# One core, two transformer blocks in fp32: block 2's attention as a pipeline over query tiles, filter taps on ScalarE and adding DMAs

## The chip, the cores and the metric

The kernel runs on one core of a Trainium2 chip. The metric is the device time of one execution in microseconds. Three runs of the kernel before took 1311.97, 1314.42 and 1315.54 us; the median, 1314.42 us, is the time before. PE is TensorE, DVE VectorE, ACT ScalarE, POOL GpSimd, SP SyncE; PSUM is the memory that matmuls write, in eight banks of 512 fp32 columns per partition.

## The reference

Two blocks follow one another on a sequence of 512 tokens, 1024 wide, in fp32. The change lies in the mixer of block 2, whose input is `u = h @ w_in`, 2560 columns, cut into four parts of which each gives 256 columns of the output:

```python
y_a = conformer_conv_mixer(u_conf, ...)   # val * sigmoid(gate), 31-tap causal depthwise convolution,
                                          # group norm over 4 x 64 channels, silu
y_b = short_conv_mixer(u_sc, ...)         # b * (3-tap convolution of c * x)
y_c = moba_attention(u_att)               # 4 heads of 64, causal, softmax with a slope per head on the distance
y_d = rglru_mixer(u_lru, ...)             # 4-tap convolution, two block-diagonal gates, a = exp(log_a),
                                          # mult = sqrt(1 - a*a), linear recurrence over tokens, times gelu(gate)
y = jnp.concatenate([y_a, y_b, y_c, y_d], axis=-1) @ w_out
```

With 512 tokens there are two blocks of 256 keys and one past block is always chosen, so the attention is plain causal attention.

## The kernel before

Every fp32 operand of a large product is split into a high and a low half of type fp32r (`split`, line 111: ACT copies the high half, DVE subtracts it to get the low half), and a product is three matmuls: high with high, high with low, low with high (lines 138 to 140, 223 to 227). A projection "chunk" gives 128 columns of `u`, channels on the partitions and 512 tokens in the free dimension: eight k-steps of three matmuls into one PSUM bank (`cm_phase`), and an `evac` function that reads the bank. The weight of a chunk is split when its turn comes (`split_w`, `wh` and `wl`, five buffers). Weights come in blocks of 256 columns on SP's queue, into three `raw` buffers.

In the mixer the eight PSUM banks have roles: three for products (`mm`, used in turn: 0, 1, 2), two for scores (`s`), two for transposes (`pt`), one for the weighted sum (`o`). H3 is the split input of the output projection, eight chunks of 128 channels: 0 and 1 the 31-tap convolution, 2 and 3 the short one, 4 and 5 the attention, 6 and 7 the recurrence.

Order of the program: five chunks (two gates and two values of the convolution, the first gelu gate); then four chunks for queries and keys and a token-major product for the values (`tm_block`); then the four heads. `at_head` goes over the four tiles of 128 queries: two matmuls of scores, DVE adds slope and mask and takes the maximum, ACT takes Exp with its sum, DVE the reciprocal and the scaling (line 1187), PE transposes the tile block by block into PSUM, and DVE or ACT copies it to `apts` (line 1191). The weighted sum follows, four fp32 products per head (line 1241). After each head some of the remaining nine chunks run (`cuts`), after heads 0 and 1 one of the two recurrences (`lru`), after head 2 the convolution's mean, after head 3 its norm.

The 62 taps of the 31-tap convolution (2 x 128 channels) are DVE instructions that wait in a list, `bg`; `pump(n)` puts n of them into the program behind a chunk. The recurrence's product of `a` with itself is written into the PSUM tile of the gate (line 1164).

The program is not run in this order. The framework lists the instructions of each engine by a planner that simulates the program and takes, among the instructions whose inputs are there in the simulation, the one that was traced first; semaphores then keep the data right. An engine runs its own list in order. `tc.keep_in_program_order(ins)`, new in the change, puts `ins` behind the instruction that was traced before it on the same engine.

Behind the mixer comes the output projection (`tm_phase`, lines 1284 and 1285): all eight banks, two per tile of 128 tokens, tiles 0 and 1 first, k-chunks in the order 6, 7, 2, 3, 4, 5, 0, 1.

Of the kernel before, what the change touches and what calls it, by code (L numbers as in the profile page):

```python
# [8 lines left out]
F32 = mybir.dt.float32  # L9
F32R = mybir.dt.float32r  # L10
AF = mybir.ActivationFunctionType
OP = mybir.AluOpType
# [3 lines left out]
P = 128  # L16
T = 512
NT = T // P
D = 1024
KC = D // P  # L20
# [6 lines left out]
NEG = -1.0e30  # L27
# [14 lines left out]
def tile_two_blocks(ctx: ExitStack, tc: tile.TileContext, a: dict, out: bass.AP, dbg=None):  # L42
# [3 lines left out]
    def open_pool(name, side="left", space=None, bufs=1):  # L46
        kw = {"space": space} if space is not None else {"side": side}
        return tc.alloc_tile_pool(name=name, bufs=bufs, reuse_waits="tile", **kw)

    def bcast_rows(ap, n):  # L50
        return bass.AP(tensor=ap.tensor, offset=ap.offset, ap=[[0, n]] + [list(d) for d in ap.ap])
# [30 lines left out]
    ident = consts.tile([P, P], F32, name="ident")  # L82
# [69 lines left out]
    def pump(n):  # L152
        for _ in range(min(n, len(bg))):
            bg.pop(0)()
# [872 lines left out]
    for g in range(2):  # L1027
        pool.memset(gmean[64 * g:64 * g + 64, 64 * g:64 * g + 64], 1.0 / 64.0)
    def tmp():
        return mx.tile([P, T], F32, name="tmp", tag="tmp", bufs=6)  # L1030

    zp = [mx.tile([P, 30 + T], F32, name=f"zp{c}") for c in range(2)]
    th_g = {}
# [19 lines left out]
    def aq_evac(c):  # L1053
        def f(ps):
            for e in range(2):
                q, r = aq(2 * c + e), HALF[e]
                act.activation(q[r, :], ps[r, :], AF.Copy, scale=qscale[r, c:c + 1])
                dve.scalar_tensor_tensor(q[HALF[1 - e], :], ps[r, :], qscale[r, c:c + 1], q[r, :].bitcast(F32),
                                         op0=OP.mult, op1=OP.subtract)
        return f  # L1060

    def ak_evac(c):
        def f(ps):
            for e in range(2):
# [7 lines left out]
    cs, cx = {}, {}  # L1072

    def sc_c(c):
        def f(ps):
            cs[c], cx[c] = tmp(), tmp()
            act.activation(cs[c], ps, AF.Copy)
        return f

    def sc_x(c):  # L1080
        def f(ps):
            dve.tensor_mul(cx[c], cs[c], ps)
            w = pv[:, c, SCW:SCW + 3]
            act.activation(cs[c], cx[c], AF.Copy, scale=w[:, 2:3])
            for j in (1, 0):
                s = 2 - j
                dve.scalar_tensor_tensor(cs[c][:, s:], cx[c][:, :T - s], w[:, j:j + 1], cs[c][:, s:],
                                         op0=OP.mult, op1=OP.add)
        return f

    def sc_b(c):
        def f(ps):
            dve.tensor_mul(cx[c], cs[c], ps)
            split(H3[0][:, 2 + c, :], H3[1][:, 2 + c, :], cx[c])
        return f

    gl = {}
# [15 lines left out]
    lg = col_blocks(w_in2, 2304, 256)  # L1113
    acc = [mx.tile([P, T], F32, name=f"cacc{c}") for c in range(2)]

    def taps(c):
        z, w = zp[c], half[:, c, :]
        bg.append(lambda: dve.tensor_scalar(acc[c], z[:, 0:T], w[:, 0:1], pv[:, c, DWB:DWB + 1],
                                            op0=OP.mult, op1=OP.add))
        for j in range(1, 31):  # L1120
            bg.append(lambda j=j: dve.scalar_tensor_tensor(acc[c], z[:, j:j + T], w[:, j:j + 1], acc[c],  # L1121
                                                           op0=OP.mult, op1=OP.add))

    sq, var = {}, {}

    def conf_mean():
        for c in (1, 0):
# [20 lines left out]


    def lru(c):  # L1150
        ths, lps = [], []
        for i in range(2):
            ps = psm.tile([P, T], F32, name="lps", tag="mm", bufs=3)
            pe.matmul(ps, bd[:, i, c, :], xc[c], start=True, stop=True)
            th = tmp()
            act.activation(th, ps, AF.Tanh, scale=0.5, bias=lbh[:, c, i:i + 1])
            ths.append(th)
            lps.append(ps)
# [12 lines left out]
        split(H3[0][:, 6 + c, :], H3[1][:, 6 + c, :], xc[c])  # L1171

    def at_head(h):
        pts = m2.tile([P, NT, T], F32, name="apts", tag="apts", bufs=1)
        for i in range(NT):
            n = (i + 1) * P
            s = psm.tile([P, T], F32, name="as", tag="s", bufs=2)
            m = max(n, 256)
            for j in range(2):
                pe.matmul(s[:, :m], aq(h)[:, i * P:(i + 1) * P], ak(h)[j][:, :m], start=j == 0, stop=j == 1)  # L1180
            L = m2.tile([P, T], F32, name="aL", tag="aL", bufs=2)
            st = m2.tile([P, 3], F32, name="ast", tag="ast", bufs=4)
            dve.tensor_tensor_reduce(L[:, :n], s[:, :n], ab[:, T - n:], scale=-0.25 ** (h + 1), scalar=-NEG,
                                     op0=OP.add, op1=OP.min, accum_out=st[:, 0:1])
            act.activation(L[:, :n], L[:, :n], AF.Exp, scale=-1.0, bias=st[:, 0:1], accum_out=st[:, 1:2])
            dve.reciprocal(st[:, 2:3], st[:, 1:2])
            dve.tensor_scalar(L[:, :n], L[:, :n], st[:, 2:3], None, op0=OP.mult)
            pt = psm.tile([P, NT, P], F32, name="apt", tag="pt", bufs=2)
            for kb in range(i + 1):
                pe.transpose(pt[:, kb, :], L[:, kb * P:(kb + 1) * P], ident)  # L1190
            (act.copy if i % 2 else dve.tensor_copy)(pts[:, 0:i + 1, i * P:(i + 1) * P], pt[:, 0:i + 1, :])
        return pts
# [4 lines left out]
    for c in (1, 0):  # L1197
        taps(c)
    dump("x3", X)
    lnp.release()  # L1200
    psm = Banks(mm=(0, 1, 2), s=(3, 4), pt=(5, 6), o=(7,))
# [10 lines left out]
    akp = m2.tile([P, 2, 2, T], F32R, name="akp")  # L1212

    def aq(h):
        return H3[h % 2][:, 4 + h // 2, :]

    def ak(h):
        return [H3[i][:, h, :] if h < 2 else akp[:, h - 2, i, :] for i in range(2)]

    av = m2.tile([P, NT, 256], F32, name="av")  # L1220
    def av_evac(t0, ps):
        act.activation(av[:, t0:t0 + 2, :], ps.rearrange("p (u c) -> p u c", u=2), AF.Copy)
        pump(RATE)

    RATE = 5
# [3 lines left out]
    rest = chunks[5:]  # L1229
    for c in range(2):  # L1230
        rest += [(sc[c], sc_c(c)), (sx[c], sc_x(c)), (sb[c], sc_b(c))]
    cuts = (0, 3, 4, 6, len(rest))


    for c in range(2):
        o = psm.tile([P, T], F32, name="ao", tag="o", bufs=1)
        for e in range(2):
            h = 2 * c + e
            pts = at_head(h)
            for kb in range(NT):  # L1240
                pe.matmul(o[64 * e:64 * e + 64, kb * P:], av[:, kb, h * 64:(h + 1) * 64], pts[:, kb, kb * P:],
                          start=kb == 0, stop=kb == NT - 1)
            cm_phase(*MM, rest[cuts[h]:cuts[h + 1]], X3, 0, rate=RATE)
            if h in (0, 1):
                lru(h)
            if h == 2:
                pump(len(bg))
                conf_mean()
            if h == 3:
                conf_norm()  # L1250
        split(H3[0][:, 4 + c, :], H3[1][:, 4 + c, :], o)
    dump("h3h", H3[0].bitcast(F32))
    m2.release()
    mx.release()
# [145 lines left out]
```

## Time and profile before

| | |
|---|---|
| median of 3 runs | 1314.42 us (1311.97 to 1315.54) |
| the profiled execution | 1314.05 us, span 1312.3 us |
| PE busy | 1294.6 us (99%), 6856 matmuls |
| DVE, ACT, POOL busy | 744.0 us (57%), 533.6 us (41%), 79.3 us (6%) |
| granted TensorE clock | 0.997 of full speed |
| block 2's mixer | 754 to 904 us of the span; its output projection 904 to 952.7 |

A profile shows one execution. Busy time is the time in which an engine works on an instruction; matmuls overlap one another, so the time from one start to the next is what a matmul costs. "Idle before" is time in which an engine stood still before an instruction, and what ended that idle time stands behind the arrow. Shares are of the whole span; what bounds a stretch has to be read from the stretch.

### The profile page before, as it was taken

The page shows a single profiled execution, that of the slowest core. Times are in us where ns is not written, and L with a number is a line of the kernel's source. Part 1 is how long each engine was busy: PE and PEld are TensorE (multiplying, and loading weights), DVE is VectorE, ACT ScalarE, POOL GpSimd, SP SyncE. Part 2 cuts the span into 40 slices and gives each one's busy share as a digit, 9 for nine tenths or more (in the row PEclk, how much of TensorE's full clock was granted, in tenths as well). Part 3 has the DMA queues.
Part 4 walks back from the last instruction along what each step waited for, and adds up shares of the span by engine and source line. Part 5 has one row for each costly group of instructions (what it writes and reads, how often), then busy time and mean ns, then how long its engine had stood idle before and what let it go on. Part 6 is the DMA issues. An engine that isn't in the chain of part 4 may idle for free.

```text
span 1312.3 us, 16931 instructions
## 1 busy us (share of the span) xinstructions
PE 1294.6 (99%) x6856; PEld 1107.5 (84%) x6856; DVE 744.0 (57%) x1202; ACT 533.6 (41%) x893; POOL 79.3 (6%) x152
## 2 busy tenths in 40 slices
PE   9999999999999999999999999899999999999998
PEld 8899899899889888888888898677898888888886
DVE  6765876576476655566533669996453334532432
ACT  5764464234333333344432234566432223431321
POOL 3220120110010000000000110000100000000000
PEclk9999999999999999999999999999999999999999
DMA  8322344534034332322223124112223332223211
GB/s 268 98 70 68 113 139 159 197 127 161 0 118 137 108 104 93 100 96 97 96 97 128 33 77 152 65 45 87 79 89 120 96 96 97 97 97 112 96 42 56
DMA packets 92447, 134.87 MB, mean 103 GB/s; under 512 B 4627, under 2 KB 77645, under 8 KB 92369
## 3 DMA queue, kind: packets, MB, share of 16 engines
q1 hardware_dynamic: 88560, 128.53, 29.7%
q10 hardware_dynamic: 3153, 3.14, 0.7%
q0 software_dynamic: 656, 2.12, 0.5%
q8 instruction: 54, 0.88, 0.3%
q14 instruction: 24, 0.20, 0.0%
HBM read 131.66 MB, written 2.12 MB: 102 GB/s over the span
## 4 chain that ended last, share of the span: by engine, by line
PE 92%; DVE 4%; ACT 1%; issue 1%; POOL 1%; DMA 0%; ACTq 0%; DVEq 0%; POOLq 0%
PE cm L139 15%; PE cm L138 15%; PE cm L140 15%; PE tm L223 9%; PE tm L224 9%; PE tm L227 9%; PE tmc L200 2%; PE tmc L201 2%; PE tmc L199 2%; PE tr L294 1%; PE tm L140 1%; PE tm L138 1%; PE tm L139 1%; DVE wl L113 1%; PE num L675 1%; DVE cacc L1121 1%
## 5 line engine op out<-in xcount | busy, mean ns | idle before, releaser
L113 DVE TENSOR_TENSOR wl<-rawc,wh 128x1024 fp32r<-128x1024 f32 x140 | 170.6, 1221 | 203.6 <-ACT wh L112 203.0
L112 ACT ACTIVATE wh<-rawc 128x1024 fp32r<-128x1024 f32 x140 | 147.8, 1059 | 244.7 <-PE cm L139 193.2
L113 DVE TENSOR_TENSOR wl<-rawr,wh 128x1024 fp32r<-128x1024 f32 x73 | 88.9, 1223 | 154.3 <-ACT wh L112 154.2
L112 ACT ACTIVATE wh<-rawr 128x1024 fp32r<-128x1024 f32 x73 | 77.0, 1059 | 182.6 <-PE tm L227 125.9
L139 PE MATMUL cm<-x2l,wh 128*128 128x512 f32 (+1 forms) x392 | 144.0, 368 | 0.0
L140 PE MATMUL cm<-x2h,wl 128*128 128x512 f32 (+1 forms) x392 | 143.8, 367 | 0.0
L138 PE MATMUL cm<-x2h,wh 128*128 128x512 f32 (+1 forms) x392 | 143.1, 368 | 0.0
L139 PE MATMUL cm<-x4l,wh 128*128 128x512 f32 (+1 forms) x296 | 106.6, 361 | 1.3 <-DVE x4l L113 1.3
L140 PE MATMUL cm<-x4h,wl 128*128 128x512 f32 (+1 forms) x296 | 106.4, 360 | 0.0
L138 PE MATMUL cm<-x4h,wh 128*128 128x512 f32 (+1 forms) x296 | 105.9, 361 | 0.0
L139 PEld LDWEIGHTS cm<-x2l,wh 128*128 128x128 f32 x392 | 73.8, 188 | 12.4 <-DVE x2l L113 0.2
L140 PEld LDWEIGHTS cm<-x2h,wl 128*128 128x128 f32 x392 | 73.8, 188 | 12.3
L138 PEld LDWEIGHTS cm<-x2h,wh 128*128 128x128 f32 x392 | 73.4, 188 | 12.0
L619 DVE SCALAR_TENSOR_TENSOR uy<-cm,fw,uy 128x511 f32<-128x511 f32 x88 | 65.5, 746 | 1.4
L138 PE MATMUL cm<-x3h,wh 128*128 128x512 f32 (+1 forms) x184 | 63.6, 351 | 1.1 <-DVE xc L619 0.8
L139 PE MATMUL cm<-x3l,wh 128*128 128x512 f32 (+1 forms) x184 | 64.3, 351 | 0.0
L139 PEld LDWEIGHTS cm<-x4l,wh 128*128 128x128 f32 x296 | 55.8, 189 | 9.9 <-DVE x4l L113 1.5
L140 PE MATMUL cm<-x3h,wl 128*128 128x512 f32 (+1 forms) x184 | 64.0, 349 | 0.0
L140 PEld LDWEIGHTS cm<-x4h,wl 128*128 128x128 f32 x296 | 55.8, 189 | 8.4
L138 PEld LDWEIGHTS cm<-x4h,wh 128*128 128x128 f32 x296 | 55.5, 189 | 8.4
L317 POOL TENSOR_TENSOR rs_r<-rs_e,mhalf 128x1 f32<-128x1 f32 (+1 forms) x16 | 26.4, 1652 | 534.2 <-DVE rs_e L316 534.2
L200 PE MATMUL tmc<-wl,xh 128*128 128x256 f32 (+1 forms) x160 | 46.6, 291 | 0.7 <-DVE wl L113 0.7
(460 smaller groups left out, 3037.3 us busy)
## 6 DMA issues: line engine op xcount, KB each, us to landing
rawc<-in_ffn_w_up_dram SPq DMA_DIRECT2D x22, 1024.0 KB
rawc<-in_w_in_dram SPq DMA_DIRECT2D x20, 1024.0 KB
rawc<-in_mlp_w_dram SPq DMA_DIRECT2D x16, 1024.0 KB
rawr<-in_mlp_w_dram SPq DMA_DIRECT2D x16, 1024.0 KB
rawr<-in_ffn_w_down_dram SPq DMA_DIRECT2D x11, 1024.0 KB
rawr<-in_w_out_dram SPq DMA_DIRECT2D x10, 1024.0 KB
rawc<-in_xa_wkv_dram SPq DMA_DIRECT2D x8, 1024.0 KB
rawc<-in_xa_wq_dram SPq DMA_DIRECT2D x4, 1024.0 KB
```

The source lines that it names most:

```text
L112: act.activation(hi, src, AF.Copy)
L113: dve.tensor_sub(lo, src, hi.bitcast(F32))
L138: pe.matmul(ps, wh, xh, start=first, stop=False)
L139: pe.matmul(ps, wh, xl, start=False, stop=False)
L140: pe.matmul(ps, wl, xh, start=False, stop=last)
L199: pe.matmul(o, xh, wh, start=k == 0, stop=False)
L200: pe.matmul(o, xh, wl, start=False, stop=False)
L223: pe.matmul(ps[t][h], xh, wh[:, c], start=i == 0, stop=False)
L224: pe.matmul(ps[t][h], xh, wl[:, c], start=False, stop=False)
L227: pe.matmul(ps[t][h], xl, wh[:, c], start=False, stop=i == n - 1)
L317: pool.tensor_tensor(r, t, mhalf[:, :n], op=OP.pow)
L619: dve.scalar_tensor_tensor(dst[:, s:], ps[:, :T - s], w[:, j:j + 1], y[:, s:], op0=OP.mult, op1=OP.add)
```

## The change

- The attention becomes one loop over 16 units (4 heads x 4 query tiles). Unit u issues its scores, then its share of the 72 k-steps of the nine remaining chunks (`stream`, 4.5 per unit), then the transposes of unit u - 2, and at every second unit the weighted sum of the two tiles before. The scores, k-steps, transposes and sums are each kept in program order.
- The weights' scaling by the reciprocal moves from DVE to ACT. The transposed weights and the values are split in fp32r halves (ACT and DVE); the halves of a head's values lie side by side in 128 columns, so one matmul against the high weights and one against the low ones, of 256 columns, give four products; the two halves of the result are added by an ACT copy and a DVE addition of 64 partitions.
- The keys of heads 2 and 3 lie in chunks 2 and 3 of H3 instead of in `akp`, so the short convolution's last factor (`sb`) moves to the end of the stream. The chunks of the recurrence's input come first.
- Nine of the 31 taps of channels 128 to 255 become ACT copies with a scale, kept in program order, one after each of the four query and key chunks and each half of the values, one before them, two in units 0 and 2. The first writes `accd`; each of the other eight writes one of two `ctap` buffers, which a DMA from POOL's queue adds to `accd`. DVE adds `accd` to the other taps' sum before the mean.
- The recurrence's square is an ACT instruction into SBUF. `tmp` has five buffers, not six.
- The convolution's mean and norm stand behind the loop.

```diff
-        dve.tensor_mul(lps[0], av_, av_)
-        dve.scalar_tensor_tensor(tn, lps[0], 1.0, tn, op0=OP.add, op1=OP.mult)
+        a2 = tmp()
+        act.activation(a2, av_, AF.Square)
+        dve.scalar_tensor_tensor(tn, a2, 1.0, tn, op0=OP.add, op1=OP.mult)
...
+    NDMA = 8
+    accd = mx.tile([P, T], F32, name="caccd")
+
+    def act_tap(j):
+        z, w = zp[1], half[:, 1, :]
+        first = j == 30 - NDMA
+        t = accd if first else mx.tile([P, T], F32, name="ctap", tag="ctap", bufs=2)
+        in_order(act.activation(t, z[:, j:j + T], AF.Copy, scale=w[:, j:j + 1]))
+        if not first:
+            pool.dma_start(accd, t, accum_op=OP.add)
...
+    RATE = 6
     ATT = [(aqs[c], aq_evac(c)) for c in range(2)] + [(aks[c], ak_evac(c)) for c in range(2)]
-    cm_phase(*MM, ATT, X3, 0, rate=RATE)
+    for chunk in ATT:
+        cm_phase(*MM, [chunk], X3, 0, rate=4)
+        next_act_tap()
     tm_block(w_in2, 1792, X3, NT, *MM, av_evac)
+    rest = chunks[6:] + [chunks[5]] + [(sc[0], sc_c(0)), (sx[0], sc_x(0)), (sc[1], sc_c(1)), (sx[1], sc_x(1)),
+                         (sb[0], sc_b(0)), (sb[1], sc_b(1))]
+    def stream():
+        for n, (src, evac) in enumerate(rest):
+            w = split_w(src())
+            ps = psm.tile([P, T], F32, name="cm", tag="mm", bufs=3)
+            for k in range(KC):
+                for i, (wi, xi) in enumerate(((0, 0), (0, 1), (1, 0))):
+                    in_order(pe.matmul(ps, w[wi][:, k, :], X3[xi][:, k, :], start=k == 0 and i == 0,
+                                       stop=k == KC - 1 and i == 2))
+                if k == KC - 1:
+                    evac(ps)
+                if (n, k) in ((1, 3), (2, KC - 1)):
+                    lru(n - 1)
+                yield
...
+    def at_scores(h, i):
...
+        dve.reciprocal(st[:, 2:3], st[:, 1:2])
+        act.activation(L[:, :n], L[:, :n], AF.Copy, scale=st[:, 2:3])
+        Ls[h, i] = L
+
+    def at_turn(h, i):
+        L = Ls.pop((h, i))
+        pt = psm.tile([P, NT, P], F32, name="apt", tag="pt", bufs=2)
+        for kb in range(i + 1):
+            in_order(pe.transpose(pt[:, kb, :], L[:, kb * P:(kb + 1) * P], ident))
+        d = ptp[i // 2][:, :, 0:i + 1, (i % 2) * P:(i % 2 + 1) * P]
+        split(d[:, 0], d[:, 1], pt[:, 0:i + 1, :])
+
+    def at_sum(h, p):
+        if p == 0:
+            os_[h] = psm.tile([P, T], F32, name="ao", tag="o", bufs=1)
+        o = os_[h]
+        for kb in range(2 * p + 2):
+            for i in range(2):
+                in_order(pe.matmul(o[:, p * 256:(p + 1) * 256], av[:, kb, h, :], ptp[p][:, i, kb, :],
+                                   start=kb == 0 and i == 0, stop=kb == 2 * p + 1 and i == 1))
...
+    for u in range(N + 3):
+        if u < N:
+            at_scores(*units[u])
+        upto = min((u + 1) * len(rest) * KC // N, len(rest) * KC)
+        for _ in range(upto - done):
+            next(filler)
+        done = upto
+        if 2 <= u < N + 2:
+            at_turn(*units[u - 2])
+        if u >= 4 and u % 2 == 0:
+            at_sum(units[u - 3][0], units[u - 3][1] // 2)
+        if u in (0, 2):
+            next_act_tap()
+        pump(1 if u < 3 else 2)
+    for _ in filler:
+        pass
+    pump(len(bg))
+    conf_mean()
+    conf_norm()
```

## Rows read from the trace of the kernel before

**Rows 1.** Busy us of each engine in four stretches, then granted clock, DMA, GB/s.
```profile
786.00:824.60 38.60, 38.60 (x239) 34.84 (x238) 37.82 (x58) 21.03 (x31) 0.00 (x0) 1.00 0.41 136
824.60:904.00 79.40, 74.69 (x324) 55.21 (x322) 67.34 (x137) 44.50 (x76) 0.00 (x0) 0.98 0.20 67
904.00:952.70 48.70, 48.70 (x222) 39.18 (x221) 26.31 (x35) 27.32 (x51) 3.57 (x5) 1.00 0.28 86
...
860.00:870.00 10.00, 10.00 (x47) 7.74 (x46) 10.00 (x23) 8.76 (x15) 0.00 (x0) 1.00 0.30 103
```
**Rows 2.** PE's waits: waiting line, releaser, us in total, times, longest.
```profile
PE apt L1190 <- DVE aL L1187: 2.3, 1, 2.3
...
PE ao L1241 <- DVE apts L1191: 1.3, 1, 1.3
...
PE cm L138 <- DVE xc L619: 0.8, 1, 0.8
```
**Rows 3.** The stretch behind those waits: us, PE busy, granted clock, DMA, GB/s.
```profile
854.40:858.10 3.70, 3.70 (x10) 0.55 0.00 0
```
**Rows 4.** Timeline of PE: start, us, instruction; three pairs of neighbours.
```profile
871.12 2.37 PE L1241 MATMUL ao<-apts,av 128*64 128x512 f32 x8
873.42 0.91 PE L1180 MATMUL as<-akp,h3h 128*128 128x384 f32 x3
...
812.71 0.28 PE L199 MATMUL tmc<-wh,x3h 128*128 128x256 f32 x1
812.83 0.28 PE L200 MATMUL tmc<-wl,x3h 128*128 128x256 f32 x1
...
858.83 0.39 PE L138 MATMUL cm<-x3h,wh 128*128 128x512 f32 x1
859.06 0.39 PE L139 MATMUL cm<-x3l,wh 128*128 128x512 f32 x1
```
**Rows 5.** Groups by form from 824.6 to 904: busy us, mean ns | idle before.
```profile
L1121 DVE SCALAR_TENSOR_TENSOR cacc<-zp,half,cacc 128x512 f32<-128x512 f32 x29 | 20.7, 739 | 0.0
...
L1187 DVE TENSOR_SCALAR aL<-aL,ast 128x512 f32<-128x512 f32 x4 | 1.9, 478 | 0.0
...
L1084 ACT ACTIVATE tmp<-tmp,pv 128x512 f32<-128x512 f32 x2 | 1.4, 706 | 0.0
...
L1164 DVE TENSOR_TENSOR lps<-tmp 128x512 f32<-128x512 f32 x2 | 1.4, 685 | 0.0
...
L1187 DVE TENSOR_SCALAR aL<-aL,ast 128x128 f32<-128x128 f32 x3 | 0.8, 280 | 0.0
```
**Rows 6.** Timeline of ACT and DVE: the second four-tap convolution, first and last pass.
```profile
843.52 0.76 ACT L616 ACTIVATE xc<-cm,pv 128x512 f32<-128x512 f32 x1
...
853.60 0.74 DVE L619 SCALAR_TENSOR_TENSOR xc<-cm,pv,xc 128x509 f32<-128x509 f32 x1
```
**Rows 7.** Timeline of ACT: the second gelu gate.
```profile
832.42 1.28 ACT L1102 ACT_TABLE_LOAD   x1
833.72 0.60 ACT L1102 ACTIVATE tmp<-cm 128x512 f32<-128x512 f32 x1
```
**Rows 8.** DMA issues on POOL's queue: count, KB each, median us to landing.
```profile
swb<-vfwd_d POOLq DMA_DIRECT2D x1, 1024.0 KB, 9.1
...
mb<-mrow_d POOLq DMA_DIRECT2D x4, 256.0 KB, 3.5
```
**Rows 9.** Timeline of POOL: two powers on 128x1.
```profile
256.40 3.72 POOL L317 TENSOR_TENSOR rs_r<-rs_e,mhalf 128x1 f32<-128x1 f32 x1 [28.42 <-DVE rs_e L316]
...
930.31 0.54 POOL L980 TENSOR_TENSOR ssr<-ssv,mhalf 128x1 f32<-128x1 f32 x1 [156.80 <-PE tm L227]
```
**Rows 10.** Timeline of PE, DVE and ACT about the output projection's start.
```profile
902.68 1.88 PE L1137 MATMUL cva<-tmp,gmean 128*128 128x512 f32 x4
...
913.10 1.29 DVE L113 TENSOR_TENSOR h3l<-cacc,h3h 128x512 fp32r<-128x512 f32 x2
...
914.43 2.96 ACT L112 ACTIVATE wxh<-rawr 128x1024 fp32r<-128x1024 f32 x3
```

More of the change, by code (lines that the diff above doesn't have):

```diff
@@ L48, in open_pool @@
         return tc.alloc_tile_pool(name=name, bufs=bufs, reuse_waits="tile", **kw)
+    in_order = tc.keep_in_program_order
     def bcast_rows(ap, n):
@@ L1029, in tmp @@
     def tmp():
-        return mx.tile([P, T], F32, name="tmp", tag="tmp", bufs=6)
+        return mx.tile([P, T], F32, name="tmp", tag="tmp", bufs=5)
     zp = [mx.tile([P, 30 + T], F32, name=f"zp{c}") for c in range(2)]
@@ L1070, in ak_evac @@
         return f
-    cs, cx = {}, {}
+    cs = {}
     def sc_c(c):
         def f(ps):
-            cs[c], cx[c] = tmp(), tmp()
+            cs[c] = tmp()
             act.activation(cs[c], ps, AF.Copy)
@@ L1081, in f @@
         def f(ps):
-            dve.tensor_mul(cx[c], cs[c], ps)
+            cx = tmp()
+            dve.tensor_mul(cx, cs[c], ps)
             w = pv[:, c, SCW:SCW + 3]
-            act.activation(cs[c], cx[c], AF.Copy, scale=w[:, 2:3])
+            act.activation(cs[c], cx, AF.Copy, scale=w[:, 2:3])
             for j in (1, 0):
                 s = 2 - j
-                dve.scalar_tensor_tensor(cs[c][:, s:], cx[c][:, :T - s], w[:, j:j + 1], cs[c][:, s:],
+                dve.scalar_tensor_tensor(cs[c][:, s:], cx[:, :T - s], w[:, j:j + 1], cs[c][:, s:],
                                          op0=OP.mult, op1=OP.add)
@@ L1092, in f @@
         def f(ps):
-            dve.tensor_mul(cx[c], cs[c], ps)
-            split(H3[0][:, 2 + c, :], H3[1][:, 2 + c, :], cx[c])
+            dve.tensor_mul(cs[c], cs[c], ps)
+            split(H3[0][:, 2 + c, :], H3[1][:, 2 + c, :], cs[c])
         return f
@@ L1114, in tile_two_blocks, with next_act_tap, taps @@
     acc = [mx.tile([P, T], F32, name=f"cacc{c}") for c in range(2)]
[L1116 to L1122, printed above, removed]
+    NDMA = 8
[7 more added lines that the diff above has]
+            pool.dma_start(accd, t, accum_op=OP.add)
+    act_taps = iter(range(30 - NDMA, 31))
+    def next_act_tap():
+        for j in act_taps:
+            act_tap(j)
+            return
+    def taps():
+        for c in (0, 1):
+            z, w = zp[c], half[:, c, :]
+            bg.append(lambda z=z, w=w, c=c: dve.tensor_scalar(acc[c], z[:, 0:T], w[:, 0:1], pv[:, c, DWB:DWB + 1],
+                                                              op0=OP.mult, op1=OP.add))
+            for j in range(1, 30 - NDMA if c else 31):
+                bg.append(lambda z=z, w=w, c=c, j=j: dve.scalar_tensor_tensor(
+                    acc[c], z[:, j:j + T], w[:, j:j + 1], acc[c], op0=OP.mult, op1=OP.add))
     sq, var = {}, {}
     def conf_mean():
-        for c in (1, 0):
+        dve.tensor_add(acc[1], acc[1], accd)
+        for c in (0, 1):
             ps = psm.tile([P, T], F32, name="cmu", tag="mm", bufs=3)
@@ L1150, in lru @@
     def lru(c):
-        ths, lps = [], []
+        ths = []
         for i in range(2):
@@ L1157, in lru @@
             ths.append(th)
-            lps.append(ps)
         tn = tmp()
@@ L1171, in lru @@
         split(H3[0][:, 6 + c, :], H3[1][:, 6 + c, :], xc[c])
[L1173 to L1192, printed above, removed]
     chunks = ([(cg[c], cgate_evac(c)) for c in range(2)] + [(cv[c], cval_evac(c)) for c in range(2)]
@@ L1196, in tile_two_blocks @@
     cm_phase(psl, "mm", 8, chunks[:5], X3, SK, fin)
-    for c in (1, 0):
-        taps(c)
+    taps()
+    next_act_tap()
     dump("x3", X)
@@ L1210, in tile_two_blocks @@
         pool.memset(qscale[64 * (h % 2):64 * (h % 2) + 64, h // 2:h // 2 + 1], 0.125 * 4.0 ** (h + 1))
-    akp = m2.tile([P, 2, 2, T], F32R, name="akp")
     def aq(h):
@@ L1217, in ak @@
     def ak(h):
-        return [H3[i][:, h, :] if h < 2 else akp[:, h - 2, i, :] for i in range(2)]
-    av = m2.tile([P, NT, 256], F32, name="av")
+        return [H3[i][:, h, :] for i in range(2)]
+    av = m2.tile([P, NT, 4, P], F32R, name="av")
     def av_evac(t0, ps):
-        act.activation(av[:, t0:t0 + 2, :], ps.rearrange("p (u c) -> p u c", u=2), AF.Copy)
+        v = av[:, t0:t0 + 2].rearrange("p u h d -> p (u h) d")
+        split(v[:, :, 0:64], v[:, :, 64:P], ps.rearrange("p (u d) -> p u d", d=64))
@@ L1223, in av_evac @@
         pump(RATE)
-    RATE = 5
+        next_act_tap()
+    RATE = 6
     ATT = [(aqs[c], aq_evac(c)) for c in range(2)] + [(aks[c], ak_evac(c)) for c in range(2)]
-    cm_phase(*MM, ATT, X3, 0, rate=RATE)
+    for chunk in ATT:
+        cm_phase(*MM, [chunk], X3, 0, rate=4)
+        next_act_tap()
     tm_block(w_in2, 1792, X3, NT, *MM, av_evac)
[L1229 to L1232, printed above, removed]
@@ L1235, in tile_two_blocks @@
[L1235 to L1251, printed above, removed]
+    rest = chunks[6:] + [chunks[5]] + [(sc[0], sc_c(0)), (sx[0], sc_x(0)), (sc[1], sc_c(1)), (sx[1], sc_x(1)),
+                         (sb[0], sc_b(0)), (sb[1], sc_b(1))]
@@ new lines, in tile_two_blocks @@
+    filler = stream()
+    ptp = [m2.tile([P, 2, 2 * p + 2, 256], F32R, name=f"apts{p}") for p in range(2)]
+    for p in range(2):
+        pool.memset(ptp[p][:, :, 2 * p + 1, 0:P].bitcast(F32), 0.0)
+    Ls, os_, osum = {}, {}, {}
+    def at_scores(h, i):
+        n = (i + 1) * P
+        s = psm.tile([P, T], F32, name="as", tag="s", bufs=2)
+        m = max(n, 256)
+        for j in range(2):
+            in_order(pe.matmul(s[:, :m], aq(h)[:, i * P:(i + 1) * P], ak(h)[j][:, :m], start=j == 0, stop=j == 1))
+        L = m2.tile([P, T], F32, name="aL", tag="aL", bufs=3)
+        st = m2.tile([P, 3], F32, name="ast", tag="ast", bufs=4)
+        dve.tensor_tensor_reduce(L[:, :n], s[:, :n], ab[:, T - n:], scale=-0.25 ** (h + 1), scalar=-NEG,
+                                 op0=OP.add, op1=OP.min, accum_out=st[:, 0:1])
+        act.activation(L[:, :n], L[:, :n], AF.Exp, scale=-1.0, bias=st[:, 0:1], accum_out=st[:, 1:2])
+        dve.reciprocal(st[:, 2:3], st[:, 1:2])
+        act.activation(L[:, :n], L[:, :n], AF.Copy, scale=st[:, 2:3])
+        Ls[h, i] = L
@@ new lines, in at_turn @@
+    def at_turn(h, i):
[13 more added lines that the diff above has]
+                                   start=kb == 0 and i == 0, stop=kb == 2 * p + 1 and i == 1))
+        if p == 1:
+            c, e = h // 2, h % 2
+            if e == 0:
+                osum[c] = tmp()
+            r = osum[c][HALF[e], :]
+            act.copy(r, o[HALF[1 - e], :])
+            dve.tensor_add(r, o[HALF[e], :], r)
+            if e == 1:
+                split(H3[0][:, 4 + c, :], H3[1][:, 4 + c, :], osum[c])
@@ new lines, in tile_two_blocks @@
+    units = [(h, i) for h in range(4) for i in range(NT)]
+    N = len(units)
+    done = 0
+    for u in range(N + 3):
[10 more added lines that the diff above has]
+        if u in (0, 2):
+            next_act_tap()
+        pump(1 if u < 3 else 2)
```

## The prediction

> **What bounds the kernel now.** I read the busy times by stretch first [rows 1]. From 786 to 952.7 us of the span, which is block 2's mixer with its output projection, PE is busy for 38.60 of 38.60 us, then 74.69 of 79.40, then 48.70 of 48.70. So TensorE sets the time before and after the attention, and 79.40 - 74.69 = 4.7 us of idle time lie inside it, between 824.6 and 904. There DVE is busy for 67.34 us and ACT for 44.50; from 860 to 870 PE and DVE are full at once and ACT has 8.76 of 10. Next I read PE's waits [rows 2]: three of them, 2.3 + 1.3 + 0.8 = 4.4 us, lie in that stretch and each ends on DVE (the scaled scores `aL`, the copied transposes `apts`, the convolution `xc`). Then the granted clock [rows 3]: right behind those idles it is 0.55 for 3.70 us, most of that at the lower of the two levels (1.2, not 2.4 GHz). At full clock the same work takes 3.70 x 0.55 = 2.0 us, so 1.7 us are lost. In all 4.7 + 1.7 = 6.4 us of the stretch are not work at full speed; that, and what the change takes from PE's own work, is all that can be won.
>
> **The change part by part.** The sum is made against the profiled execution, 1314.05 us (span 1312.3 and 1.75 around it); the median of the runs, 1314.42, is 0.4 above it.
>
> *The weighted sum.* Before, four fp32 products per head, two records each, take 873.42 - 871.12 = 2.30 us [rows 4]. After, the values and the weights are split in fp32r halves, the halves of the values side by side in 128 columns: 4 + 8 = 12 matmuls of 256 columns per head. Such a matmul starts 0.12 us after the one before it (812.71, 812.83) [rows 4], so 1.44 us. Gain 4 x 0.86 = 3.4 us of PE, on the path since PE is what ends everything here. Scores, transposes and the 72 steps of three matmuls are as many as before.
>
> *The old waits.* Scores now run two units (query tiles) ahead of their transposes, and the sum one unit behind. A unit is about (79.4 - 6.4 - 3.4) / 16 = 4.4 us of PE, so the chain reduce, Exp, reciprocal, scale has some 8 us where it had none. The waits on `aL` and `apts` go, and with the wait on `xc` and the slow clock I book -6.4 us, and put back what follows.
>
> *What is late next.* The order of PE is fixed now, so a wait can't be filled. PSUM's three `mm` banks rotate: the two projections to the recurrence's input take banks 0 and 1, the recurrence's gates 2 and 0, so the third projection gets bank 1 again at once, and its first matmul stands behind the whole convolution of the second: one ACT pass and three DVE passes that read this bank. Their durations are 0.76 and 0.74 [rows 6], so alone about 0.76 + 3 x 0.67 + hand-overs = 3.0 us of PE idle. Before, the same chain ran from 843.52 to 854.34, 10.8 us, for DVE was full and ran filter taps in between [rows 6]; only 0.8 of that reached PE, because other work stood in front. Ends 3.0 and 10.8; I take 3.5, for nine taps have left DVE, and the rest were spread thin there (one per unit). The fourth projection has bank 1 too, behind the gelu: table load 1.28 and pass 0.60 [rows 7], of which the second recurrence's two gate products hide some 1.7: 0.2 to 2, I take 0.5. The first recurrence's gates stand behind the first convolution, with four steps (2.7 us) in front: 0 to 3, I take 0.5. Together +4.5, bounds 3.2 and 16. If the clock falls behind this gap as it did before, 1.7 more [rows 3]; I book none, since PE works in full up to it.
>
> *DVE.* Nine taps of 0.74 (6.7 us), the 16 scalings of 0.28 to 0.48 (6 us) and two squares of 0.68 leave it [rows 5]; the low halves of 16 transposed tiles (8 of them were plain copies here) and of the values, four half sums and one addition come, 8 to 9 us. So about 5 us less in a stretch with 67. DVE isn't the path by itself, hence 0 (bounds -1 and +1).
>
> *ACT.* Nine taps and 16 scalings with a scale per row (0.71 at 512 columns) [rows 5], two squares, eight copies that DVE had and four half sums: about 20 us, 15 of them in the attention: 60 of some 74 us. Off the path, cost 0, while it lags less than the 8 us of a pipeline's two units. In 860 to 870 it had 8.76 of 10 [rows 1]; with 15/74 = 0.2 per us on top it lacks 0.8 us in ten while the recurrences run (some 25 us): 2 us of lag. The square in SBUF frees the gates' PSUM bank earlier, which nobody waited for: 0.
>
> *The adding DMAs.* Eight, one behind another on `accd`, from POOL's queue, which stood idle for 156.80 us up to 930 [rows 9]. An ACT tap is pinned; it waits for one of two `ctap` buffers, and behind it stand all evacuations of ACT. Taps follow the chunks' 24 matmuls, 5.5 us apart from about 797 on; the last two come in units 0 and 2. The nearest rows: a POOL DMA of 256 KB lands after 3.5 us, one of 1024 KB after 9.1 [rows 8]. An adding one reads its target too; I take 5: no wait, 0 us. At 9.1 us it is the rival below.
>
> *Queues and tail.* SP issues the same loads; the block with the second gate projection is held in one of three raw buffers some 5 us longer, and the loads behind it have a whole projection (5.4 us) in hand: 0. The mean and norm of the convolution now follow the attention. From the variance to the split it took 902.68 to 914.4 [rows 10], beside the output projection from 904 on; with the mean in front it will be some 17 us. The projection's other six k-chunks, for four tiles, are 24 x 6 matmuls of 0.23 = 33 us of PE [rows 4], so it is hidden, but the last weight splits (at 914.43 before) and the first tiles end later. I take +0.5, bounds 0 and 3.
>
> Sum: -3.4 - 6.4 + 4.5 + 0.5 = -4.8; 1314.05 - 4.8 = 1309.3 us.
>
> **A rule against it.** One form of POOL instruction, a power on 128x1, has rows of 0.54 and of 3.72 us [rows 9], so POOL can be held up by something on this core. The Trainium skill, SBUF — State Buffer, "Who interferes with whom", says that a DVE instruction in a two-port mode locks GpSimd out of a shared port for its whole length, and that descriptors GpSimd makes for DMAs starve by it. By that rule the eight DMAs would each start late beside a full DVE, and the time would be the third rival's; no row before shows a POOL DMA beside a DVE as full as in 786 to 880.
>
> **The rivals.** *The wait moves (same).* The fixed order gives back what it takes: the convolution's chain costs 5 to 6, gelu and gates 1.5, the clock falls for 1.7. For it: the 10.8 us chain, and that no work is free to fill in. Against: DVE is lighter. -9.8 + 5 to 6 + 1.5 + 1.7 + 0.5 = -1.1 to -0.1: about 1313.5.
>
> *ACT becomes the bound (slower).* Place: units 2 to 7, with both recurrences, the gelu and their table loads of 1.28 each among the Exps. If each Exp of a unit brings a load of its own (six more, 7.7 us), the lag is 2 + 7.7 = 9.7 us, past the 8 us that decide; from there each us of ACT is one of PE, and evacuations are late too: some 12 to 15 us beside the 4.5, 1321 to 1324. Against: ACT was idle for 35 of the 79 us [rows 1].
>
> *The DMA blocks ACT (slower).* From about 7 us a landing: the taps after the fourth wait. At 9.1 us the adds end 9.1 apart from 797, the sixth at 852, while the last tap is wanted two units after 824.6, at 833: ACT stands for about 19 us in all, less 8 of slack, 10 us of PE: 1319.
>
> *Nearly all is won.* The convolution's chain runs at 3.0 with the gates' wait inside it and the gelu hidden: -9.8 + 3.2 + 0 = 1307.4.
>
> **How the numbers follow.** 0.3% (3.9 us: 1310.5 and 1318.4) is about what a measurement of this kernel can tell from no change. Forecast, 1307.8 to 1310.5: 0.37. Nearly all won, below 1307.8: 0.15. The wait moves, 1310.5 to 1316: 0.27. ACT: 0.12. DMA: 0.09, of which and of ACT 0.17 lie beyond 1318.4 and 0.04 within. So faster 0.52, same 0.31, slower 0.17. The range 1304.5 to 1319 leaves out some 0.05 below and 0.15 above; the forecast's own range is 1307.8 to 1310.5.
>
> **What would show it.** Twelve `ao` matmuls of 0.12 us per head; no PE wait on `aL` or on the transposes' copies; one PE wait of 3 to 4 us on `xc` at the third projection of the stream, a smaller one on the gelu; the clock at full level; `accd` DMAs that land under 5.5 us; ACT at 80% in the attention; the output projection begins some 5 us earlier and ends so. Wrong is the forecast if PE waits for `aL` or for ACT's evacuations unit by unit, if ACT's taps wait on DMAs, if PE idles in the output projection for the convolution's chunks, or if the convolution's chain takes over 6 us.

## The result and the profile after

The changed kernel took 1332.23 us (median of 4 runs, 1330.5 to 1334.32) against 1314.18 of the kernel before in the same comparison: a ratio of 1.0138, 95% interval 1.0126 to 1.0151. It is slower. Its profiled execution has a span of 1328.7 us, 16.4 more than before.

The first view is PE's waits in the attention, 824 to 890 us (waiting line and releaser: us in total, times, longest). Lines 1179, 1249, 621 and 1105 are those of the changed kernel: gates, stream, four-tap convolution, gelu.

```profile
PE lps L1179 <- issue: 9.7, 1, 9.7
PE cm L1249 <- DVE xc L621: 7.0, 1, 7.0
PE cm L1249 <- ACT tmp L1105: 3.2, 1, 3.2
```

They add up to 19.9 us, where [rows 2] had 4.4 (4.7 of idle time in [rows 1]). The waits on `aL` and `apts` of [rows 2] are gone. PE's timeline has the same three as idle time in brackets; the third row is the second recurrence's gate products, the last one seven matmuls of a weighted sum.

```profile
842.61 3.75 PE L1179 MATMUL lps<-xc,bd 128*128 128x512 f32 x4 [9.69 <-issue]
...
857.58 0.77 PE L1249 MATMUL cm<-x3h,wh 128*128 128x512 f32 x1 [6.98 <-DVE xc L621]
...
864.59 1.88 PE L1179 MATMUL lps<-xc,bd 128*128 128x512 f32 x4
...
871.77 0.50 PE L1249 MATMUL cm<-x3h,wh 128*128 128x512 f32 x1 [3.23 <-ACT tmp L1105]
...
931.28 0.99 PE L1292 MATMUL ao<-apts,av 128*128 128x256 f32 x7
```

The same gate products took 3.75 us behind the long wait and 1.88 without one. The windows (length; busy us of PE, weight loads, DVE, ACT, POOL; granted clock; DMA share; GB/s) give the clock behind each wait:

```profile
842.60:848.40 5.80, 5.79 (x11) 3.20 (x12) 5.40 (x9) 2.59 (x5) 0.00 (x0) 0.51 0.00 0
857.50:862.00 4.50, 4.42 (x13) 3.60 (x14) 1.85 (x5) 1.67 (x3) 0.00 (x0) 0.51 0.00 0
871.70:875.00 3.30, 3.23 (x8) 2.56 (x9) 0.69 (x1) 3.27 (x6) 0.00 (x0) 0.57 0.00 0
```

At 0.51 of full speed (nearly the lower level, 1.2 of 2.4 GHz) these stretches lose 5.79 x 0.49 + 4.42 x 0.49 + 3.23 x 0.43 = 6.4 us. So the account closes to within half a us: idle and slow clock 19.9 + 6.4 = 26.3 us against the 4.7 + 1.7 = 6.4 of the prediction, 19.9 more; the weighted sum gives 3.4 back; 16.5, and the span has grown by 16.4.

The timelines of ACT and DVE show what each wait stood behind. For the first: pinned taps that waited for their DMAs, then the first convolution's pass on ACT and its last pass on DVE, after which the gates could start.

```profile
829.78 0.72 ACT L1128 ACTIVATE ctap<-zp,half 128x512 f32<-128x512 f32 x1 [3.43 <-DMA caccd<-ctap]
833.59 0.72 ACT L1128 ACTIVATE ctap<-zp,half 128x512 f32<-128x512 f32 x1 [1.27 <-DMA caccd<-ctap]
835.45 0.76 ACT L618 ACTIVATE xc<-cm,pv 128x512 f32<-128x512 f32 x1
```

```profile
841.65 0.74 DVE L621 SCALAR_TENSOR_TENSOR xc<-cm,pv,xc 128x509 f32<-128x509 f32 x1
```

For the second, the second convolution's pass on ACT and its last pass on DVE; for the third, the weight split, the table load and the gelu:

```profile
851.55 0.76 ACT L618 ACTIVATE xc<-cm,pv 128x512 f32<-128x512 f32 x1
...
868.36 1.06 ACT L114 ACTIVATE wh<-rawc 128x1024 fp32r<-128x1024 f32 x1
...
869.83 1.28 ACT L1105 ACT_TABLE_LOAD   x1
871.12 0.60 ACT L1105 ACTIVATE tmp<-cm 128x512 f32<-128x512 f32 x1
```

```profile
856.71 0.72 DVE L621 SCALAR_TENSOR_TENSOR xc<-cm,pv,xc 128x509 f32<-128x509 f32 x1
```

The group of the adding DMAs (KB each, median us to landing); the one issued at 824.64 took longest, 5.05 us, and it is the one behind the wait of 3.43.

```profile
caccd<-ctap POOLq DMA_DIRECT2D x8, 256.0 KB, 3.3
```

### The profile page after: what moved, and what is told of

Read it like the earlier page. It is cut to its first block, busy times and chain, and to the rows that moved or that the text cites. A ratio compares the mean times of both kernels' runs of the same rounds, so it can differ in the third digit from the quotient of the medians.

```text
span 1328.7 us, 17002 instructions
## 1 busy us (share of the span) xinstructions
PE 1296.1 (98%) x6872; PEld 1112.4 (84%) x6872; DVE 742.3 (56%) x1190; ACT 557.4 (42%) x934; POOL 83.4 (6%) x162
## 4 chain that ended last, share of the span: by engine, by line
PE 93%; ACT 2%; DVE 2%; DMA 2%; issue 1%; ACTq 0%; DVEq 0%; POOLq 0%
PE cm L141 14%; PE cm L140 14%; PE cm L142 14%; PE tm L225 9%; PE tm L226 9%; PE tm L229 9%; PE cm L1249 3%; PE tmc L202 2%; PE tmc L203 2%; PE tmc L201 2%; PE tr L296 1%; DMA caccd<-ctap 1%; PE tm L142 1%; PE tm L141 1%; PE tm L140 1%; PE num L677 1%
## 5 line engine op out<-in xcount | busy, mean ns | idle before, releaser
L201 PE MATMUL tmc<-wh,xh 128*128 128x256 f32 (+1 forms) x160 | 45.9, 287 | 0.5 <-ACT wh L114 0.5
L203 PE MATMUL tmc<-wh,xl 128*128 128x256 f32 (+1 forms) x160 | 46.0, 288 | 0.0
L1249 PE MATMUL cm<-x3h,wh 128*128 128x512 f32 x72 | 30.6, 425 | 10.2 <-DVE xc L621 7.0
```

The costliest lines, as they stand in the source:

```text
L201: pe.matmul(o, xh, wh, start=k == 0, stop=False)
L203: pe.matmul(o, xl, wh, start=False, stop=k == KC - 1)
L1249: in_order(pe.matmul(ps, w[wi][:, k, :], X3[xi][:, k, :], start=k == 0 and i == 0, stop=k == KC - 1 and i == 2))
```

## The experiments

Ratios are against the kernel before, measured beside it on the same chip, with a 95% interval. The changed kernel's is 1.0138. The kernel before itself had medians of 1314.18 to 1315.60 us in the four comparisons, so a difference in us between kernels of different comparisons is good to 1 or 2 us.

**Which part costs: DMAs, banks, pinned taps, square.** The first and the fourth of these undo a part of the change, the second and the third alter one. The first puts all taps on DVE.

```diff
-    accd = mx.tile([P, T], F32, name="caccd")
...
-    act_taps = iter(range(30 - NDMA, 31))
+    act_taps = iter(())
...
-            for j in range(1, 30 - NDMA if c else 31):
+            for j in range(1, 31):
...
-        dve.tensor_add(acc[1], acc[1], accd)
```

> All 31 taps of channels 128 to 255 on DVE again; no ACT taps, no adding DMAs, the rest as changed. Theory A (ACT stands behind the adding DMA, so the recurrence's convolution is evacuated late): the 9.7 us wait of PE falls below 3 us, the 7.0 us wait to 3 or 4, the clock stays up: 1332 - 16 = about 1316 us. Theory B (the third and fourth projection get the PSUM bank that the convolution and the gelu still read): the waits of 7.0 and 3.2 us stay or grow, for DVE has 6.7 us more: 1322 us or more.

1329.64 us, 1.0112 (1.0097 to 1.0127). PE's waits, in its own line numbers:

```profile
PE cm L1247 <- DVE xc L621: 9.2, 1, 9.2
PE lps L1177 <- issue: 5.7, 1, 5.7
PE cm L1247 <- ACT tmp L1105: 3.2, 1, 3.2
```

The gates' wait falls from 9.7 to 5.7 since ACT stands behind no DMA, and the next wait, with nine more taps on DVE, grows from 7.0 to 9.2. The taps on ACT with their DMAs cost 2.6 us (0.26% by the ratios, whose intervals just touch), not the loss.

The second puts the gates into the banks of the transposes; in the kernel before they stood in the `mm` banks too.

```diff
-            ps = psm.tile([P, T], F32, name="lps", tag="mm", bufs=3)
+            ps = psm.tile([P, T], F32, name="lps", tag="pt", bufs=2)
```

> Only the recurrence's gate products go to the transposes' PSUM banks, so the projections rotate through all three banks and none gets the one just left. Theory A: the late ACT still holds the gates, whose wait (9.7 us) stays, and what stood behind the convolution waits there instead: 1327 to 1332 us. Theory B: the waits of 7.0 and 3.2 us go: about 1321 us, the 9.7 stays.

1320.11 us, 1.0035 (1.0021 to 1.005), 12 us less, as theory B said.

```profile
PE lps L1179 <- issue: 11.3, 2, 9.1
PE ao L1292 <- ACT apts L114: 0.4, 1, 0.4
```

With the gates out of the rotation the third and fourth projections no longer meet a bank in use: the waits on the convolution and the gelu are gone. The gates' own wait stays (9.1 at the first recurrence, 2.2 at the second).

The third lets the scheduler place ACT's taps.

```diff
-        in_order(act.activation(t, z[:, j:j + T], AF.Copy, scale=w[:, j:j + 1]))
+        act.activation(t, z[:, j:j + T], AF.Copy, scale=w[:, j:j + 1])
```

> The nine ACT taps are no longer kept in program order; the planner lists them earlier and farther apart (all before 815 us or so), the DMAs are the same. Theory A: ACT no longer waits on a DMA between 824 and 834, the 9.7 us wait falls below 4: 1317 to 1321 us. Theory B: 1327 us or more, since the banks are as before.

1338.87 us, 1.0182 (1.0166 to 1.0197). The premise of the expectation, taps farther apart, was a miss. Waits of 6.8, 5.1 and 3.2 stay, and a new one comes ahead of the attention:

```profile
PE tmc L201 <- DVE h3l L1069: 8.4, 1, 8.4
```

Unpinned, the taps are listed closer together, run into the DMAs earlier (ACT waits for them for 15.1 us in all, against 5.4 in the changed kernel), and delay the key evacuations behind them on ACT. An adding DMA does block ACT; the pin had kept the worst of it away.

The fourth puts the recurrence's square back on DVE and into PSUM.

```diff
+            lps.append(ps)
...
-        a2 = tmp()
-        act.activation(a2, av_, AF.Square)
-        dve.scalar_tensor_tensor(tn, a2, 1.0, tn, op0=OP.add, op1=OP.mult)
+        dve.tensor_mul(lps[0], av_, av_)
+        dve.scalar_tensor_tensor(tn, lps[0], 1.0, tn, op0=OP.add, op1=OP.mult)
```

> Only the recurrence's square goes back to DVE and the gate's PSUM bank. Theory A: nothing near 824 to 857 us hangs on it: 1330 to 1334 us. Theory B: the gate's bank is held some us longer, but no projection wants it before two more: 1330 to 1334 us as well; a slower run, 1336 or more, would say that the square's place mattered for a bank.

1333.51 us, 1.0141 (1.0125 to 1.0156): the interval overlaps the changed kernel's. No difference from the square's place is to be seen.

**Where the recurrences stand.** Three kernels move them later. The fifth is the second with this edit, the sixth is the fifth with the first's edit as well, and the seventh has this edit alone.

```diff
-                if (n, k) in ((1, 3), (2, KC - 1)):
-                    lru(n - 1)
+                if (n, k) in ((2, 3), (3, 3)):
+                    lru(n - 2)
```

> Gate products in the transposes' banks, and the two recurrences 8 and 4 k-steps later in the stream (behind step 4 of the third and of the fourth projection). Theory B (PE's fixed order stands behind the first convolution and behind the reused bank, and nothing else is wrong with the pipeline): the 9.1 us wait of the gates shrinks by the 8 steps (5.4 us) to 4 or less, the clock falls less: 1320 - 7 = 1311 to 1314 us. Theory A (ACT late through the adding DMAs): the lateness moves on to the next evacuation, 1317 us or more.

> As the run before, and all taps on DVE, no adding DMAs. Theory A: 3 us or more faster than the run before (the 4 us between the gates' waits of 9.7 and 5.7 us). Theory B: DVE's nine more taps (6.7 us) lie between the passes of the convolution instead, so within 2 us of the run before, either side.

> Only the two recurrences later; the gates stay in the three product banks. The rotation is now: inputs 0 and 1, third projection 2, gates 0 and 1, fourth 2 again (behind the gelu) and so on. Theory B: the gates' wait shrinks to 4 or less and the 7.0 us wait goes, for the third projection has a bank of its own; the 3.2 us wait behind the gelu stays: 1332 - 5.4 - 7 = 1317 to 1321 us. Theory A: 1327 us or more.

e5: 1316.0 us, 1.0011 (1.0001 to 1.0021), between its two ranges; the gates wait for 4.7 us, `aL` for 1.8. e6: 1313.09 us, 0.9978 (0.9968 to 0.9987): 0.2% faster than the kernel before. Its waits are 4.1 us at the gates and 0.8 elsewhere. Between e5 and e6 lie the nine taps on ACT with their DMAs: 2.9 us, 0.33%, just under the 3 us of theory A. e7: 1329.4 us, 1.0107 (1.0092 to 1.0122), where theory B said 1317 to 1321, a miss (theory A's 1327 or more holds the time): with the gates in the `mm` banks a later place moves the wait to the next bank (7.7 at the gates, 3.6 and 3.1 on ACT's evacuations, 2.2 on `aL`).

**What makes the second convolution late.** My reading after these runs was that filter taps between its DVE passes do; e8 and e9 each take one kind of neighbour away. e8 leaves out 58 of the 62 taps, with all ACT taps and DMAs; e9 leaves out the recurrences and splits the plain convolutions into H3 in their place.

The diff has e8's loop first (the rest of its edit is the first kernel's) and e9's step second, where the banks still rotate.

```diff
-            for j in range(1, 30 - NDMA if c else 31):
+            for j in range(1, 2):
...
-                    lru(n - 1)
+                    psm.roles["mm"] = psm.roles["mm"][2:] + psm.roles["mm"][:2]
```

> 58 of the 62 taps of the 31-tap convolution are left out, with the ACT taps and the DMAs among them, the rest as changed; DVE is idle much of the time. It measures the convolution's chain with nothing in between. If the chain's length is DVE's taps (my size of 3.0 us alone): the bank's wait falls from 7.0 to about 3.0 us, the gates' from 9.7 to 1 or less, the gelu's stays at 3.2. If the chain is long by hand-overs and ACT instead: the two waits stay above 5 us.

> Both recurrences are left out (gates, Tanh, Exp, Square, Sqrt, scan; their output is the plain convolution); the rotation of the banks is as with them, and filter taps, adding DMAs and the fixed order of PE are as in the changed kernel. Theory R (the passes of the second convolution stand behind instructions of the first recurrence on ACT and DVE): PE's wait on the convolution at the third projection falls from 7.0 to 2 to 4 us. Theory T (filter taps and key evacuations make that convolution long): it stays at 6 to 7. Nothing else of the chain can shorten it. Its time says little, since two recurrences less are also some 7 us of PE less.

One run each, so without an interval: 1320.85 and 1323.64 us. Without taps the gates' wait falls from 9.7 to 2.2: with e1's 5.7, that makes some 4 us of it the taps on ACT with their DMAs and some 3.5 the taps on DVE. PE's wait on the second convolution stays:

```profile
PE cm L1247 <- DVE xc L621: 7.7, 1, 7.7
```

DVE's timeline of e8 shows the three passes (line 621) between instructions of the first recurrence:

```profile
841.14 0.69 DVE L1188 SCALAR_TENSOR_TENSOR tmp<-tmp 128x512 f32<-128x512 f32 x1 [0.36 <-ACT tmp L1187]
843.22 0.74 DVE L621 SCALAR_TENSOR_TENSOR xc<-cm,pv,xc 128x511 f32<-128x511 f32 x1
845.30 0.69 DVE L1191 TENSOR_TENSOR tmp<-tmp 128x512 f32<-128x512 f32 x1 [1.33 <-ACT tmp L1189]
845.91 0.74 DVE L621 SCALAR_TENSOR_TENSOR xc<-cm,pv,xc 128x510 f32<-128x510 f32 x1
846.57 1.21 DVE L1192 TENSOR_TENSOR_SCAN xc<-tmp 128x512 f32<-128x512 f32 x1
847.70 0.72 DVE L621 SCALAR_TENSOR_TENSOR xc<-cm,pv,xc 128x509 f32<-128x509 f32 x1
```

DVE is not full there: before 845.30 it stands idle for 1.33 us, for an instruction of the recurrence that waits for ACT, with the second pass listed behind it.

Without recurrences there is no wait for gates, and the other one grows, against both theories: it now holds both convolutions, 13.0 us where 9.7 + 7.0 stood. PE's wait in e9, and the window in which it falls:

```profile
PE cm L1249 <- DVE xc L621: 13.0, 1, 13.0
```

```profile
839.00:852.20 13.20, 0.29 (x2) 0.00 (x0) 11.57 (x23) 5.33 (x12) 1.72 (x2) 0.66 0.64 197
```

In that window DVE is busy for 11.57 of 13.20 us, with taps now, and of the rest it waits 1.63 us for the last adding DMA, ahead of the last pass. So for this wait neither neighbour alone is the cause: whichever is left stands in DVE's list between the passes, and PE pays for all of it because it may do nothing else. That points to PE's order.

**PE's order.** The tenth kernel frees stream steps, scores, transposes and sums in this way (the stream's first line is shown); ACT's taps stay pinned.

```diff
-    in_order = tc.keep_in_program_order
+    in_order, free = tc.keep_in_program_order, lambda i: i
...
-                    in_order(pe.matmul(ps, w[wi][:, k, :], X3[xi][:, k, :], start=k == 0 and i == 0,
+                    free(pe.matmul(ps, w[wi][:, k, :], X3[xi][:, k, :], start=k == 0 and i == 0,
...
```

> The changed kernel, but the scheduler may order scores, transposes, sums and stream steps on PE by itself; the ACT taps are still pinned. Theory F (the fixed order of PE is what turns late convolutions into idle time): the waits on the convolution, the gates and the gelu are filled with scores and transposes, 8 to 15 of the 20 us go, 1317 to 1324. Rival (the buffers leave nothing to fill in: two score banks, three aL, one bank for the projections): PE waits as long, in other places: 1329 to 1335.

1315.96 us, 1.0006 (0.9997 to 1.0016): 16 us less, the whole loss and more than the 8 to 15 expected, with the same banks, buffers, taps and DMAs. PE's timeline, where the changed kernel had its two waits of 9.7 and 7.0:

```profile
836.50 0.38 PE L1282 MATMUL apt<-ident,aL 128*128 128x128 f32 x2
...
838.97 0.39 PE L1268 MATMUL as<-h3h,h3l 128*128 128x256 f32 x1 [1.85 <-DVE ast L1271]
...
841.42 0.50 PE L1268 MATMUL as<-h3h,h3l 128*128 128x384 f32 x1 [1.95 <-DVE ast L1271]
...
844.58 3.75 PE L1179 MATMUL lps<-xc,bd 128*128 128x512 f32 x4 [1.49 <-issue]
...
850.97 0.50 PE L1249 MATMUL cm<-x3h,wh 128*128 128x512 f32 x1 [1.13 <-DVE xc L621]
```

The first convolution is no earlier: the gates start at 844.58 against 842.61. But by 836.50 the second projection is complete, so its convolution runs beside the first one, from 838.77 on ACT to 850.91 on DVE, and PE does scores, transposes and sums meanwhile. The third projection starts at 850.97 against 857.58. From 824.6 to 904 PE idles for 6.8 us in place of 19.9.

```profile
838.77 0.76 ACT L618 ACTIVATE xc<-cm,pv 128x512 f32<-128x512 f32 x1
```

```profile
850.17 0.74 DVE L621 SCALAR_TENSOR_TENSOR xc<-cm,pv,xc 128x509 f32<-128x509 f32 x1
```

In the changed kernel the gates are listed in the middle of the second projection: its other half waits for the first convolution, so its own convolution starts that much later, and the waits stand one behind another. The scheduler listed ACT and DVE anew for this order too, so PE's part alone isn't measured apart from that. Nor is a fixed order slow by itself: e6 keeps it and is faster than the kernel before, with the gates in other banks and later, and all taps on DVE.

**The sum alone.** e11 has all taps on DVE, the gates in the transposes' banks, and each recurrence in a step of the stream apart from convolutions and gelu; e12 is e11 with the old fp32 sum. The diff shows what comes to the edits of e1 and e2, and behind the dots the sum of e12, whose values and transposed weights are plain copies again (the transposes in turn by ACT and DVE).

```diff
-    return mx.tile([P, T], F32, name="tmp", tag="tmp", bufs=5)
+    return mx.tile([P, T], F32, name="tmp", tag="tmp", bufs=8)
...
-                if (n, k) in ((1, 3), (2, KC - 1)):
-                    lru(n - 1)
+                if (n, k) in ((3, 3), (5, 3)):
+                    lru(0 if n == 3 else 1)
...
-            for i in range(2):
-                in_order(pe.matmul(o[:, p * 256:(p + 1) * 256], av[:, kb, h, :], ptp[p][:, i, kb, :],
-                                   start=kb == 0 and i == 0, stop=kb == 2 * p + 1 and i == 1))
...
+            s = P if kb == 2 * p + 1 else 0
+            in_order(pe.matmul(o[64 * e:64 * e + 64, p * 256 + s:(p + 1) * 256], av[:, kb, h * 64:(h + 1) * 64],
+                               ptp[p][:, kb, s:], start=kb == 0, stop=kb == 2 * p + 1))
```

> All 31 taps on DVE, no adding DMAs; the recurrence's gates in the transposes' banks; its recurrences in the fourth and sixth step of the stream, one projection apart from both convolutions and from the gelu; eight tmp buffers instead of five, in the room of the DMA tap's tiles. Against the kernel with the same but recurrences in the third and fourth step (1313.09, gates' wait 4.1 us, clock 0.91 after it): if the gates' wait there comes from the second Tanh standing behind gelu and table loads on ACT, PE waits under 1.5 us in all, the clock stays at 1.0, and the time is 1315.3 - 3.4 - 6.4 + 1 to 3 = 1306 to 1309, ratio 0.994. If PE's waits simply move to the next place, 1312 to 1315.

> As the kernel before it in this call, but the weighted sum as in the kernel before the change: fp32 products, values evacuated by one ACT pass, transposes copied plainly in turn by ACT and DVE. Theory: the split sum is worth its 3.4 us of PE, so this is 3 to 4 us slower than its neighbour. Rival (PE's time in the sum is not on the path, or the low halves' DVE work costs as much): within 1 us of it.

e11: 1312.71 us, 0.998 (0.9971 to 0.9989), in the second of its two ranges: the waits moved (3.0 us at the gates, 1.7 on `apts`). e12: 1312.07 us, 0.9975 (0.9966 to 0.9984). The intervals overlap: in this arrangement the split sum brings nothing that can be measured. The windows show where its gain goes, e11 first, e12 second:

```profile
824.60:850.00 25.40, 24.51 (x122) 20.20 (x121) 25.40 (x51) 16.80 (x30) 0.00 (x0) 1.00 0.24 84
850.00:870.00 20.00, 16.37 (x72) 12.31 (x71) 16.99 (x33) 16.20 (x30) 0.00 (x0) 0.91 0.15 53
...
824.60:904.00 79.40, 74.71 (x353) 58.98 (x352) 68.85 (x137) 60.71 (x111) 0.00 (x0) 0.98 0.20 67
```

```profile
824.60:850.00 25.40, 24.28 (x114) 19.19 (x114) 24.36 (x50) 17.15 (x31) 0.00 (x0) 1.00 0.24 84
850.00:870.00 20.00, 20.00 (x90) 14.72 (x91) 18.20 (x35) 16.21 (x29) 0.00 (x0) 1.00 0.18 53
...
824.60:904.00 79.40, 78.28 (x358) 59.16 (x358) 63.42 (x126) 59.68 (x104) 0.00 (x0) 1.00 0.20 67
```

With the split sum DVE has 68.85 us to do in the stretch against 63.42 (3.1 more for the low halves of the transposed weights than for the copies, 2.0 for the half sums), and is busy for all 25.40 us of the first window. PE then idles for 4.69 us and loses some 1.5 to the clock; with the old sum it idles for 1.12 at full clock. PE's own work is 3.4 us less with the split sum, and the idle time and slow clock behind a full DVE take it back; that DVE's extra work makes this idle time is read from the windows, not tested by itself. e6, e11 and e12 are all faster than both kernels, by 0.2 to 0.25% of the kernel before, and not told apart.

## Why the prediction was wrong

It said 1309.3 us; it is 1332.23. The step that failed is the term for what is late next, and with it the clock, which it put at nothing. By its own steps:

- *The weighted sum*, -3.4: right as a term of PE (the seven matmuls above end within 0.99 us of the first one's start, and one alone lasts 0.28: 0.71 / 6 = 0.12 from start to start). That it is on the path "since PE is what ends everything here" did not hold in e11 and e12: e12 is as fast without it.
- *The old waits*, -6.4: right. No wait on `aL` or on the transposes' copies is left.
- *What is late next*, +4.5: the step that failed. Its mechanism was right, three waits at the three places that it named, but each was sized far too small: 3.5 for the third projection's bank (7.0 measured), 0.5 for the gelu (3.2), 0.5 for the first gates (9.7). The bounds given, 3.2 to 16, did not hold the 19.9. The sum did add the three waits, as a fixed list has them (e10 shows that they need not stand one behind another); what was wrong is the length of each. A convolution's chain, from the start of its pass on ACT to the end of its last pass on DVE, was taken at 3.0 us; the first took 6.9 (835.45 to 842.39), the second 5.9 (851.55 to 857.43). The prediction saw that the chain of 10.8 us of [rows 6] had reached PE with only 0.8 of it "because other work stood in front", and that the change takes that cover away, and then took the end near 3.0 because DVE had lost nine taps, with the rest "spread thin". But DVE's list is filled with whatever is ready: four taps ran between the passes of the first convolution. And the chain was taken to start at once. The first projection ended at about 830.5, and ACT, behind pinned taps with their DMAs, a table load and a weight split, began the pass 4.9 us later; less the 2.4 us of PE's work in front of the gates (four steps and the scores), that is about the 9.7. The gelu's 1.28 and 0.60 were right, but a weight split and a scaling stood in front of them on ACT, and the two gate products that were to hide 1.7 of it had already run at 864.59: they were not pinned.
- *The clock*: "I book none, since PE works in full up to it" was wrong by 6.4 us; the 1.7 that it named for one such gap would have been about a quarter of it. Each of the three idles had a stretch at 0.51 to 0.57 behind it, as [rows 3] had behind the old ones.
- *The adding DMAs*, "no wait, 0 us": the landing was better than estimated (3.3 in the median, one of 5.05, against 5), but the taps did not come 5.5 us apart. On ACT they start at 819.79, 821.20, 824.19, 829.78 and 833.59, and three of these waited, for 0.67, 3.43 and 1.27 us. The taps on ACT with their DMAs cost 2.6 us in e1 and 0.33% between e5 and e6. The rival's mechanism was at work, at a quarter of its price and from a shorter landing than its 7 us.
- *The rule against it*: not borne out. POOL issued the eight DMAs in 0.85 to 0.96 us each, three of them (801.36, 807.61 and 820.81) in a stretch (797 to 824.6) where DVE was busy for 27.19 of 27.60 us, with scalar_tensor_tensor and tensor_tensor alone; the one of 820.81 landed in 3.29 us. The Trainium skill, SBUF — State Buffer, "Who interferes with whom", speaks of DVE's two-port modes. Beside the instructions of that stretch no starving is to be seen. The landing of 5.05 us from 824.64 fell beside a DVE that was busy for 4.37 us of it; what held it is open.
- *DVE, ACT, queues and the square*: right in kind. Where the stretch runs at its old length (e10) DVE has 62.91 us and ACT 59.16 of 79.40, near the estimates of 5 us less than 67 and of 60. ACT was not the bound: no wait on evacuations unit by unit. No cost of the square is to be seen (e4).
- *The tail*, +0.5: nothing to be seen. PE has the same waits behind the output projection as before, 1.0 to 1.4 us on `x4l`, and one of 0.3 more.

The rival nearest to what happened, that the wait moves, had the mechanism and the clock but a price of 5 to 6 for the chain. Left open: e12's waits and clock are some 5 us better than before in the account above, its span only 3.3. The other 1 to 2 us lie in PE's busy time, which is 1294.6 us in both although e12 lost nothing to the clock in the attention; what fills them I have not found.

## What to carry to other kernels

Fixing one engine's order takes away what hid the chains of the others. Before pinning, list every producer that the fixed list will stand behind. Price each chain with what its engines will run between its parts (here 6.9 and 5.9 us, where the instructions alone take 3.0), add how late its first engine is (here 4.9 us), and add the waits up. Moving work from a full PE to a DVE that is nearly as full, as the split sum does, brought nothing here once DVE was full too.

## What was not expected of the hardware

The clock was lost behind each wait by itself: the three waits of 9.7, 7.0 and 3.2 us each had 3 to 6 us at about half speed behind them, so 19.9 us of idle time cost 26.3. Behind e12's one wait in the stretch, 1.1 us, nothing was lost (granted clock 1.00). An adding DMA of 256 KB within SBUF lands in 3.3 us in the median, no longer than the plain POOL DMA of that size in [rows 8], but single ones took longer: 5.05 us here, up to 7.2 in e3.
